# Dilated queries, keys and eight gate tiles by seven block products (Strassen) in an fp32 hybrid-attention layer

## The chip, the cores and the metric

The kernel runs on one core of one Trainium2 chip. The time is the device time of one execution of the program in microseconds (us), as the median of several runs. In this text, "faster" or "slower" means a difference of over 0.5% of the median before.

## What is computed

The layer takes x (1024 tokens by 1024 channels, fp32), normalises it, multiplies it by one wide input matrix and cuts the result into the operands of two attention mixers and two gates:

```python
h = rmsnorm(x, attn_norm_g)
proj = h @ w_in
(c_q, c_kv, k_rope, z_mla, q_dil, k_dil, v_dil, z_dil, g_mla, g_dil) = jnp.split(proj, ...)
a_out = mla_attention(...)                      # 8 heads, dense, 1024 by 1024 scores each
y_mla = (a_out * silu(z_mla)) @ w_o_mla
d_out = dilated_mixture(q_dil, k_dil, v_dil)    # 3 groups of 8 heads, rotary on q and k
y_dil = (d_out * silu(z_dil)) @ w_o_dil
merged = sigmoid(g_mla + b) * y_mla + sigmoid(g_dil + b) * y_dil
out = rmsnorm(x + merged @ w_out)
```

The dilated queries and keys are 2 x 1536 columns of `proj`, the two z and the two g are 2 x 512 and 2 x 1024 columns. In tiles of 128 columns that is 24 tiles of queries and keys, 8 of z and 16 of g (8 of g_mla, 8 of g_dil).

## The kernel before

**Numbers.** All matmuls are fp32 by three fp32r products: each operand is held as a high part and the remainder (`split`, L73 to L76: ScalarE casts the high part, another engine subtracts it), and `mm3` (L67 to L71) issues high x high, high x low and low x high. A projection tile (`proj_steps`) is 128 output columns by one half of the tokens (512): 8 chunks of the 1024 channels, 24 matmuls of 128x512, into one PSUM bank. One tile of 128 columns is therefore 48 such matmuls. The activations stay in SBUF as `hT_h` and `hT_l`; weights are loaded as `w_raw` (512 KB a tile), cast on ScalarE to `w_h` and subtracted on GpSimd to `w_l` (`wtile`).

**Stages.** (1) `latent_proj`. (2) `latents`, in which the latents are expanded for the dense mixer, together with the six calls of `dil_v` (values, 128x256 matmuls), whose matmuls fill the gaps of the latents. (3) `dil_qk`, 12 calls, each for two tiles (the two rotary halves of four heads): 96 matmuls of 128x512, then `rope` (L233: VectorE multiplies PSUM by cosine and sine, L234 and L235: GpSimd adds and subtracts), a split on ScalarE and GpSimd, and stores to DRAM (`s_dq`, `s_dk`). (4) `dil_attention`, (5) `mla_attention`, (6) the loop over the 16 tiles (8 column tiles by 2 halves) of `output` before the last product, (7) the last product with `w_out`.

**Fillers.** In stages 4 and 5 TensorE would wait for softmax, so a generator, `fillers`, hands out other matmuls: first the 24 tiles of z and g (16 steps of three matmuls each), then the output projection of the dilated mixer (64 steps), then three of the four parts of that of the dense mixer. `feed(n)` owes n steps at each of its call sites; `FEED` holds n for the sites, its last two numbers for the dense mixer: one after each 128-row score block (`s_mla`, L529) and one after each group of four transposes (`pt`, L543). There are 192 such calls. The generator can reach a point where it has to wait for finished heads (`mla_done`); its steps are then empty. What the fillers have not done of the output projection is left to stage 6, where each tile needs VectorE for a gate (L825), for the low part of the merged tile (`mg_l`) and for the low part of one piece of `w_out` (`wout_l`).

**Order.** The tile framework's scheduler fixes every engine's order of instructions when the program is built; on the chip each engine runs its list in order. Pools of SBUF and PSUM are a stack: a tile of a pool opened later may lie where a closed pool's tile lay, and then waits for its last reader.

Of the kernel before, what the change touches and what calls it, by code (L numbers as in the profile page):

```python
# [10 lines left out]
F32 = mybir.dt.float32  # L11
# [20 lines left out]
FEED = (1.9, 1.35, 1.2, 1.25, 2, 3, 1.1, 1.1)  # L32
# [6 lines left out]
T_ZM, T_QK = 0, 24  # L39

# [9 lines left out]
class Net:  # L50
# [16 lines left out]
    def mm3(self, out, lh, ll, rh, rl, start, stop):  # L67
        mm = self.nc.tensor.matmul
        mm(out, lh, rh, start=start, stop=False)  # L69
        mm(out, lh, rl, start=False, stop=False)  # L70
        return mm(out, ll, rh, start=False, stop=stop)  # L71
# [7 lines left out]
    def wtile(self, src, wp=None, n=8):  # L79
        raw = self.wp.tile([128, 8, 128], F32, name="w_raw")  # L80
        wp = wp or self.wp
        h = wp.tile([128, 8, 128], F32R, name="w_h")
        l = wp.tile([128, 8, 128], F32R, name="w_l")
        self.dma(raw[:, :n], src)
        self.split(raw[:, :n], h[:, :n], l[:, :n], self.nc.gpsimd)
        return h, l

    def proj_half(self, w, half, pool):

        return run_all(self.proj_steps(w, half, pool))  # L90

    def proj_steps(self, w, half, pool):

        ps = pool.tile([128, 512], F32, name="pj")
        t = slice(half * 512, half * 512 + 512)
        for kc in range(8):
            self.mm3(ps, w[0][:, kc], w[1][:, kc], self.hTh[:, kc, t], self.hTl[:, kc, t], kc == 0, kc == 7)
            if kc < 7:
                yield
        return ps  # L100
# [234 lines left out]
    def dil_v(self, g, quad, tp, pj):  # L335

        nc, a = self.nc, self.a
        w = []
        for kk in range(2):
            raw = self.wp.tile([128, 4, 256], F32, name="w_raw")  # L340
            wp = (self.wp, self.wpx)[kk]
            h = wp.tile([128, 4, 256], F32R, name="w_h")
            l = wp.tile([128, 4, 256], F32R, name="w_l")
            self.dma(raw, a["wv"][g * 2 + quad, kk])
            self.split(raw, h, l, nc.gpsimd)
            w.append((h, l))
        for t in range(8):
            ps = pj.tile([128, 512], F32, name="pj")[:, :256]
            for kc in range(8):
                wh, wl = w[kc // 4]  # L350
                sl = slice(128 * t, 128 * t + 128)
                self.mm3(ps, self.hTh[:, kc, sl], self.hTl[:, kc, sl], wh[:, kc % 4], wl[:, kc % 4], kc == 0, kc == 7)
            pv = ps.rearrange("p (h d) -> p h d", d=64)
            f = self.rcol[:, t:t + 1]
            if g < 2:
                st = tp.tile([128, 4, 2, 64], F32R, name="dv_st")
                nc.scalar.mul(st[:, :, 0], pv, f)
                nc.vector.scalar_tensor_tensor(out=st[:, :, 1], in0=pv, scalar=f, in1=st[:, :, 0].bitcast(F32), op0=ALU.mult, op1=ALU.subtract)
                x = slice(quad * 512, quad * 512 + 512)
                if g == 0:  # L360
                    dst = self.dv[0][128 * t + 64:128 * t + 192, x]
                else:

                    dst = self.dv[1].rearrange("(r m) x -> m r x", r=4)[32 * t:32 * t + 32, :, x]
                self.dma(dst, st.rearrange("p h a d -> p (h a d)"))
            else:
                st = tp.tile([128, 4, 64], F32, name="dv_s2")
                nc.scalar.mul(st, pv, f)
                self.dma(self.dv[2][128 * t:128 * t + 128, quad * 256:quad * 256 + 256], st.rearrange("p h d -> p (h d)"))

    def dil_qk(self, g, quad, which, tp, pj):

        nc, a = self.nc, self.a
        base = T_QK + (g * 2 + quad) * 4 + which * 2
        wa, wb = self.wtile(a["wt"][base]), self.wtile(a["wt"][base + 1], wp=self.wpx)
        if g < 2:
            st = [[tp.tile([128, S], F32R, name=f"dq_st{c}{p}") for p in range(2)] for c in range(2)]
        else:
            st = [[tp.tile([128, S], F32, name=f"dq_st{c}0")] for c in range(2)]
        for half in range(2):  # L380
            c512 = slice(half * 512, half * 512 + 512)
            pa, pb = self.proj_half(wa, half, pj), self.proj_half(wb, half, pj)
            o = self.rope(pa, pb, self.cos_d[:, c512], self.sin_d[:, c512], tp)
            for c in range(2):
                if g == 0:
                    self.split(o[c], st[c][0][:, c512], st[c][1][:, c512], nc.gpsimd)
                    continue
                if g == 1:
                    src = o[c].rearrange("p (m r) -> p r m", r=4)
                    dst = [x.rearrange("p (r m) -> p r m", r=4)[:, :, 128 * half:128 * half + 128] for x in st[c]]  # L390
                    self.split(src, dst[0], dst[1], nc.gpsimd)
                else:

                    src = o[c].rearrange("p (m b e) -> p e b m", b=8, e=2)
                    dst = st[c][0].rearrange("p (e b m) -> p e b m", e=2, b=8)[:, :, :, 32 * half:32 * half + 32]
                    for e in range(2):
                        nc.scalar.copy(out=dst[:, e], in_=src[:, e])
        off = 64 if (g == 0 and which) else 0
        dst = (self.dq if which == 0 else self.dk)[g]
        for c in range(2):  # L400
            for p in range(len(st[c])):
                for j in range(4):

                    self.dma(dst[quad * 4 + j, p, c, :, off:off + S], st[c][p][32 * j:32 * j + 32])
# [10 lines left out]
    def fillers(self, pj):  # L415
# [3 lines left out]
        with tc.tile_pool(name="zt", bufs=2, side="right") as tp:  # L419
            z_tile = lambda: tp.tile([128, 512], F32, name="zg_z")  # L420
            t_tile = lambda: tp.tile([128, 512], F32, name="zg_t")
            for i in [4, 5, 6, 7, 0, 1, 2, 3, *range(16, 24), *range(8, 16)]:
                w = self.wtile(a["wt"][T_ZM + i])
                for half in range(2):
                    c = slice(half * 512, half * 512 + 512)
                    ps = yield from self.proj_steps(w, half, pj)
                    z, t = z_tile(), t_tile()
                    nc.vector.tensor_tensor(out=z, in0=ps, in1=self.R[:, c], op=ALU.mult)  # L428
                    if i < 8:
                        nc.scalar.activation(out=t, in_=z, func=AF.Tanh, scale=0.5)  # L430
                        nc.gpsimd.tensor_tensor(out=t, in0=t, in1=z, op=ALU.mult)
                        nc.gpsimd.tensor_tensor(out=t, in0=t, in1=z, op=ALU.add)
                        self.dma(self.zs[i][:, c], t)
                    else:
                        nc.scalar.activation(out=t, in_=z, func=AF.Tanh, scale=0.5, bias=self.hb[:, i - 8:i - 7])
                        self.dma(self.gt[i - 8][:, c], t)
# [49 lines left out]
    def o_proj(self, i, dt, half, w, w0, js, br, t, pp, w3=None):  # L486
# [4 lines left out]
        for j in js:  # L491
            wh, wl = (x[:, dt if j == 3 and w3 else w0 + j] for x in (w3 if j == 3 and w3 else w))
# [303 lines left out]
    def output(self, pp):  # L796
        nc, a, tc = self.nc, self.a, self.tc
        v = nc.vector
        with tc.tile_pool(name="w3", bufs=1) as w3p, tc.tile_pool(name="wo", bufs=1) as wp, tc.tile_pool(name="mg", bufs=1) as mp:
            w3 = self.wtile(a["wom3"], wp=w3p)  # L800
# [64 lines left out]
    def run(self):  # L865
        tc, nc = self.tc, self.nc
        with ExitStack() as ctx:
# [23 lines left out]
            with tc.tile_pool(name="wpx", bufs=2, side="right") as self.wpx, tc.tile_pool(name="cosd", bufs=1, side="right") as dpool:  # L891
                z = dpool.tile([128, 8, 64], F32, name="zero")
                with tc.tile_pool(name="pj_a", bufs=NB_A, space=PSUM) as pj:
                    with tc.tile_pool(name="dvp", bufs=3) as vp, tc.tile_pool(name="lp", bufs=1) as lp, \
                            tc.tile_pool(name="pj_l", bufs=8 - NB_A, space=PSUM) as pl:
# [4 lines left out]
                        with tc.tile_pool(name="cosm", bufs=1) as mpool, tc.tile_pool(name="up", bufs=1) as lp:  # L900
# [5 lines left out]
                            for g in range(3):  # L906
                                for quad in range(2):
                                    self.dil_v(g, quad, vp, pj)
                    nc.vector.memset(z, 0.0)
# [3 lines left out]
                    with tc.tile_pool(name="dt", bufs=2, side="right") as tp:  # L913
                        for x in (self.cos_d, self.sin_d):
                            for half in range(2):
                                c = slice(512 * half, 512 * half + 512)
                                nc.gpsimd.tensor_tensor(out=x[:, c], in0=x[:, c], in1=self.R[:, c], op=ALU.mult)
                        for quad in range(2):
                            for g in range(3):
                                self.dil_qk(g, quad, 0, tp, pj)  # L920
                                self.dil_qk(g, quad, 1, tp, pj)
# [98 lines left out]
```

## Time and profile before

| | us |
|---|---|
| median of 3 runs (1336.35, 1343.12, 1337.54) | 1337.54 |
| the profiled execution | 1340.99 |
| its span, first to last instruction | 1339.2 |
| stage 1, 0 to 49.5 | 49.5 |
| stage 2, latents and values, 49.5 to 229.6 | 180.1 |
| stage 3, dilated queries and keys, 229.6 to 497.8 | 268.2 |
| stage 4, dilated attention, 497.8 to 822.7 | 324.9 |
| stage 5, dense attention, 822.7 to 1196.4 | 373.7 |
| stage 6, rest of the output projection, 1196.4 to 1243.4 | 47.0 |
| stage 7, product with `w_out`, 1243.4 to 1339.2 | 95.8 |

The cuts are the starts of the first `pj<-hT_h,w_h` (stage 3), `s_ps` (4), `s_mla` (5), the end of the last `av` (6) and the start of the first `pj<-wout_h` (7) on TensorE. In rows of the profile, PE is TensorE, PEld its weight load, DVE VectorE, ACT ScalarE, POOL GpSimd and SP the queue that issues the DMAs. The duration of a matmul in a row is its latency; matmuls overlap, and what one costs is the distance between starts.

### The profile page before, as it was taken

How to read it: one execution, taken by the hardware profiler on the slowest of the kernel's cores; microseconds unless marked ns; L12 is line 12 of the kernel's file. 1: busy time of each engine (PE TensorE's matmuls, PEld its weight loads, DVE VectorE, ACT ScalarE, POOL GpSimd, SP SyncE). 2: the span in 40 equal slices, each digit the busy share in tenths (PEclk: the TensorE clock that was granted, in tenths of full speed). 3: DMA queues.
4: the chain of work that ended last, by engine and by line, in shares of the span. 5: the costliest groups of instructions: out<-in, count | busy, mean ns of one | idle time of the engine just before them, and what ended most of it. 6: DMA issues, size and time to landing. Idle time of an engine off the chain costs nothing.

```text
span 1339.2 us, 19315 instructions
## 1 busy us (share of the span) xinstructions
PE 1275.4 (95%) x7101; PEld 1108.4 (83%) x7101; DVE 655.4 (49%) x1204; ACT 563.3 (42%) x1102; POOL 455.0 (34%) x302
## 2 busy tenths in 40 slices
PE   8989999999999999988989889999999999998998
PEld 8879999888888878877878777788888878886786
DVE  7483520222222224656576565656555556558622
ACT  6533332123322225545455453455554545444322
POOL 2251212576466634525422031212111022035522
PEclk9989999999999999989999999999999999999999
DMA  9747562585345535678777778545333463136322
GB/s 322 227 154 272 196 248 80 162 217 159 106 115 151 135 98 164 163 184 224 190 186 208 196 195 203 156 120 160 92 99 100 103 178 119 63 116 205 131 96 75
DMA packets 128253, 213.03 MB, mean 159 GB/s; under 512 B 36440, under 2 KB 65696, under 8 KB 126304
## 3 DMA queue, kind: packets, MB, share of 16 engines
q1 hardware_dynamic: 128160, 211.81, 54.6%
q8 instruction: 56, 0.92, 0.3%
q14 instruction: 37, 0.30, 0.1%
HBM read 143.01 MB, written 68.75 MB: 158 GB/s over the span
## 4 chain that ended last, share of the span: by engine, by line
PE 70%; DMA 9%; DVE 5%; issue 2%; SPq 1%; ACT 1%; POOL 1%; DVEq 0%; ACTq 0%; POOLq 0%
PE pj L69 17%; PE pj L70 16%; PE pj L71 16%; PE pt L543 4%; PE av L552 2%; PE av L551 2%; PE s_mla L69 2%; PE s_mla L71 2%; PE s_mla L70 2%; DMA s_sd<-av_t 2%; PE pt L642 2%; SPq L65 1%; PE av L663 1%; DMA op_a<-s_dk 1%; PE s_ps L698 1%
## 5 line engine op out<-in xcount | busy, mean ns | idle before, releaser
L69 PE MATMUL pj<-hT_h,w_h 128*128 128x512 f32 x768 | 315.0, 410 | 3.7 <-DVE zg_z L428 2.1
L76 POOL TENSOR_TENSOR w_l<-w_raw,w_h 128x1024 fp32r<-128x1024 f32 (+1 forms) x70 | 167.5, 2396 | 441.1 <-ACT w_h L75 371.4
L71 PE MATMUL pj<-hT_h,w_l 128*128 128x512 f32 x768 | 301.9, 393 | 0.0
L70 PE MATMUL pj<-hT_l,w_h 128*128 128x512 f32 x768 | 301.6, 393 | 0.0
L233 DVE TENSOR_TENSOR rope_m<-pj,cs_d 128x512 f32<-128x512 f32 x96 | 61.9, 686 | 241.1 <-PE pj L71 241.1
L76 DVE TENSOR_TENSOR pt_l<-pt,pt_h 128x512 fp32r<-128x512 f32 x192 | 131.6, 686 | 89.0 <-ACT pt_h L75 87.1
L71 PEld LDWEIGHTS pj<-hT_h,w_l 128*128 128x128 f32 x768 | 145.3, 189 | 31.5
L69 PEld LDWEIGHTS pj<-hT_h,w_h 128*128 128x128 f32 x768 | 145.8, 190 | 29.7 <-DVE zg_z L428 3.0
L75 ACT CAST pt_h<-pt 128x512 fp32r<-128x512 f32 x192 | 112.0, 584 | 130.0 <-PE pt L543 60.0
L70 PEld LDWEIGHTS pj<-hT_l,w_h 128*128 128x128 f32 x768 | 146.0, 190 | 24.4
L70 PE MATMUL pj<-w_l,hT_h 128*128 128x256 f32 x384 | 109.6, 286 | 0.0
L71 PE MATMUL pj<-w_h,hT_l 128*128 128x256 f32 x384 | 109.4, 285 | 0.0
L69 PE MATMUL pj<-w_h,hT_h 128*128 128x256 f32 x384 | 109.3, 285 | 0.0
L75 ACT CAST w_h<-w_raw 128x1024 fp32r<-128x1024 f32 (+1 forms) x70 | 72.3, 1034 | 74.5 <-PE pj L70 59.5
L529 DVE TENSOR_REDUCE m_nm<-s_mla 128x1 f32<-128x1024 f32 x64 | 78.0, 1221 | 32.6 <-PE s_mla L71 32.4
L608 ACT ACTIVATE p<-p,d_st 128x256 f32<-128x256 f32 x128 | 64.4, 505 | 60.5 <-DVE d_st L607 60.4
L532 ACT ACTIVATE p<-s_mla,m_nm 128x1024 f32<-128x1024 f32 x64 | 71.8, 1123 | 25.5 <-PE pt L543 19.2
L543 PE MATMUL pt<-consts,p 128*128 128x128 f32 x512 | 79.6, 276 | 0.0
L552 PE MATMUL av<-pt_l,op_c 128*128 128x256 f32 x256 | 67.2, 286 | 8.5 <-DVE pt_l L76 8.5
L69 PEld LDWEIGHTS pj<-w_h,hT_h 128*128 128x128 f32 x384 | 73.6, 192 | 1.1
L607 DVE CUSTOM_DVE_ANT_0 p<-s_ps,masks 128x256 f32<-128x256 f32 x128 | 51.0, 417 | 48.0 <-PE s_ps L635 27.3
L70 PEld LDWEIGHTS pj<-w_l,hT_h 128*128 128x128 f32 x384 | 73.7, 192 | 0.7
(232 smaller groups left out, 2548.4 us busy)
## 6 DMA issues: line engine op xcount, KB each, us to landing
w_raw<-wt SPq DMA_DIRECT2D x48, 512.0 KB, 4.7
op_b<-s_dq SPq DMA_DIRECT2D x32, 512.0 KB, 8.5
s_dq<-dq_st SPq DMA_DIRECT2D x80, 128.0 KB, 2.6
s_dk<-dq_st SPq DMA_DIRECT2D x80, 128.0 KB, 2.4
gate<-s_gt SPq DMA_DIRECT2D x34, 256.0 KB, 3.0
s_dv<-dv_st SPq DMA_DIRECT2D x32, 256.0 KB, 3.9
s_gt<-zg_t SPq DMA_DIRECT2D x32, 256.0 KB, 3.7
w_raw<-wv SPq DMA_DIRECT2D x12, 512.0 KB, 5.9
```

What stands on the lines that cost most here:

```text
L69: mm(out, lh, rh, start=start, stop=False)
L70: mm(out, lh, rl, start=False, stop=False)
L71: return mm(out, ll, rh, start=False, stop=stop)
L75: self.nc.scalar.copy(out=h, in_=raw)
L76: sub.tensor_tensor(out=l, in0=raw, in1=h.bitcast(F32), op=ALU.subtract)
L233: v.tensor_tensor(out=mi, in0=p, in1=tab, op=ALU.mult)
L529: v.tensor_reduce(out=nm[:, hh, qb:qb + 1], in_=s, axis=AX.X, op=ALU.max, negate=True)
L532: nc.scalar.activation(out=p, in_=s, func=AF.Exp, bias=nm[:, hh, qb:qb + 1], accum_out=den[:, hh, qb:qb + 1])
L543: self.anchor = nc.tensor.transpose(pt[:, o:o + 128], P[b2][:, 128 * kc:128 * kc + 128], self.ident)
L552: nc.tensor.matmul(a_out, vv[:, kc], pl[:, s], start=False, stop=kc == 7)
L607: nc.vector.tensor_tensor_reduce(out=p, in0=s, in1=mask, op0=ALU.add, op1=ALU.min, scale=-0.125, scalar=3e38, accum_out=nm)
L608: nc.scalar.activation(out=p, in_=p, func=AF.Exp, scale=-1.0, bias=nm, accum_out=den)
```

## The change

Two tiles of columns are computed together: the 1024 channels are cut into two halves, the 1024 tokens into two halves and the 256 columns into two tiles, so that a pair is a 2 by 2 block product. Instead of eight block products (8 x 4 chunks x 3 = 96 matmuls of 128x512), `block_pair` makes seven (84), in Strassen's form as Winograd wrote it: four sums of the blocks of x are built once for all pairs (`block_sums`: `s0` to `s3`, high and low), and for every pair four sums of weight blocks are made on GpSimd, in place in `w_raw` (`minus`). The seven weight operands are split in halves of the earlier tile size (128x512), ScalarE and GpSimd as before. The products go to four PSUM banks `st_a` to `st_d`; three copies on ScalarE (`copied`) and five additions on VectorE, which write to PSUM, put the four outputs together.

Done this way are the 12 calls of `dil_qk` and 8 of the 16 gate tiles (i = 8 to 15, those of g_mla) as 4 pairs, which leave the fillers and go into stage 3 after pairs 2, 5, 8 and 11. The rotation and the split of `dil_qk` now run on VectorE alone, in place in PSUM, and the four stores of a part become one DMA of 512 KB. The last two numbers of `FEED` go from 1.1 to 0.7. Pools move: `sums` and `bs` lie where the pools of the latents lay, and `dt`, which now holds two of the three pairs of `w_raw` in flight, lies where the values' staging pool `dvp` lay.

```diff
-FEED = (1.9, 1.35, 1.2, 1.25, 2, 3, 1.1, 1.1)
+FEED = (1.9, 1.35, 1.2, 1.25, 2, 3, 0.7, 0.7)
+ZG_PAIRS = ((8, 2), (10, 5), (12, 8), (14, 11))
...
+    def block_sums(self, sp, tp):
...
+        for kc in range(4):
...
+                    self.dma(x, a["xt"][i, :, c])
+                    nc.scalar.mul(x, x, self.ga[:, c:c + 1])
+            p.tensor_tensor(out=y[1, 1], in0=y[1, 0], in1=y[1, 1], op=ALU.add)
+            p.tensor_tensor(out=y[1, 0], in0=y[0, 0], in1=y[1, 0], op=ALU.subtract)
+            p.tensor_tensor(out=y[0, 0], in0=y[1, 1], in1=y[0, 0], op=ALU.subtract)
+            p.tensor_tensor(out=y[0, 1], in0=y[0, 1], in1=y[0, 0], op=ALU.subtract)
+            for i, x in enumerate((y[1, 1], y[0, 0], y[1, 0], y[0, 1])):
+                self.split(x, self.sh[i][:, kc], self.sl[i][:, kc], nc.vector)
...
+    def block_pair(self, first, tp, pp):
...
+            raw.append(self.wp.tile([128, 8, 128], F32, name="w_raw") if self.pairs % 3 == 0 else tp.tile([128, 8, 128], F32, name="w_raw", bufs=4))
+            self.dma(raw[i], a["wt"][first + i])
...
+        ps = {n: pp.tile([128, 512], F32, name=f"st_{n}") for n in "abcd"}
...
+        w1, w2 = operand(b[b11]), operand(b[b21])
+        minus(t1, b[0, 1], b11)
+        minus(t3, b[b22], (0, 1))
+        product("a", w1, hx(0, 0), True)
+        product("b", w2, hx(0, 1), True, True)
+        w1, w2 = operand(b[t1]), operand(b[t3])
+        minus(t2, b[b22], t1)
+        product("c", w1, sx(0), True)
+        u = copied("a")
+        v.tensor_tensor(out=ps["b"], in0=ps["b"], in1=u, op=ALU.add)
+        product("d", w2, sx(2), True)
+        w1, w2 = operand(b[b22]), operand(b[t2])
+        minus(t4, b[b21], t2)
+        u = copied("c")
+        t = tp.tile([128, 512], F32, name="st_t")
+        v.tensor_tensor(out=t, in0=ps["d"], in1=u, op=ALU.add)
+        product("a", w2, sx(1), False, True)
+        product("c", w1, sx(3), False, True)
+        product("d", operand(b[t4]), hx(1, 1), False, True)
+        u = copied("a")
+        for bank, x in (("a", t), ("c", u), ("d", u)):
+            v.tensor_tensor(out=ps[bank], in0=ps[bank], in1=x, op=ALU.add)
...
     def dil_qk(self, g, quad, which, tp, pp):
...
-            pa, pb = self.proj_half(wa, half, pj), self.proj_half(wb, half, pj)
-            o = self.rope(pa, pb, self.cos_d[:, c512], self.sin_d[:, c512], tp)
...
+            for x, y in zip(m, (pb, pa)):
+                v.tensor_tensor(out=x, in0=y, in1=sin, op=ALU.mult)
+            for x in o:
+                v.tensor_tensor(out=x, in0=x, in1=cos, op=ALU.mult)
+            for x, y, op in zip(o, m, (ALU.subtract, ALU.add)):
+                v.tensor_tensor(out=x, in0=x, in1=y, op=op)
...
-                for j in range(4):
-                    self.dma(dst[quad * 4 + j, p, c, :, off:off + S], st[c][p][32 * j:32 * j + 32])
+                self.dma(dst[quad * 4:quad * 4 + 4, p, c, :, off:off + S], st[c][p])
...
-            for i in [4, 5, 6, 7, 0, 1, 2, 3, *range(16, 24), *range(8, 16)]:
+            for i in [4, 5, 6, 7, 0, 1, 2, 3, *range(16, 24)]:
...
+                with tc.tile_pool(name="dt", bufs=1, side="right") as tp, tc.tile_pool(name="st", bufs=2, space=PSUM) as pp:
```

Counted in TensorE's list, stage 3 has 1368 matmuls of 128x512 now (1344 of the seven products and 24 of fillers) against 1176 before; the fillers have 696 in stage 4 both times, 339 against 642 in stage 5; stage 6 has 93 against 174. Together that is 192 fewer, 12 for each of 16 pairs. In stage 5, cut into its 32 blocks of 256 query rows, seven blocks have 3 fillers or none now (3, 3, 0, 0, 0, 0, 3), and three have 6; before every block had 15 to 24.

Three places in the order. First TensorE where stage 2 ends, before (the last rows of the values, then the first tile of queries):

```order
L69 MATMUL pj<-w_h,hT_h 128x256
L70 MATMUL pj<-w_l,hT_h 128x256
L71 MATMUL pj<-w_h,hT_l 128x256
L69 MATMUL pj<-hT_h,w_h 128x512
L70 MATMUL pj<-hT_l,w_h 128x512
L71 MATMUL pj<-hT_h,w_l 128x512
```

and now, with the first two block products (`st_a`, `st_b`):

```order
L73 MATMUL pj<-w_h,hT_l 128x256
L71 MATMUL st_a<-hT_h,w_h 128x512
L72 MATMUL st_a<-hT_l,w_h 128x512
L71 MATMUL st_b<-hT_h,w_h 128x512
L72 MATMUL st_b<-hT_l,w_h 128x512
L73 MATMUL st_a<-hT_h,w_l 128x512
```

The first products start on the high part of two operands, and the rows that need the low part `w_l` stand behind them.

Second, the DMA queue on SP at the same place, with what each entry waits for (DMAHW0 to 7 are the counters of completed DMAs that the queue's entries take in turn, the others count an engine's instructions). `s_dv` are the stores of the values, `w_raw<-wt` the loads of the weights of queries and keys. Before:

```order
L65 DMA s_dv_70<-dv_s_2206 128x256 [waits DMAHW1_49,Activation_49]
L65 DMA w_raw<-wt 128x1024 [waits DMAHW2_49,Pool_49]
L65 DMA s_dv_70<-dv_s_2246 128x256 [waits DMAHW3_49,Activation_49]
L65 DMA w_raw<-wt 128x1024 [waits DMAHW4_49,Pool_49]
L65 DMA s_dv_70<-dv_s_2274 128x256 [waits DMAHW5_49,Activation_49]
```

and now, the last stores of the values and the first loads:

```order
L67 DMA s_dv_70<-dv_s_2548 128x256 [waits DMAHW7_49,Activation_49]
L67 DMA s_dv_70<-dv_s_2576 128x256 [waits DMAHW0_49,Activation_49]
L67 DMA s_dv_70<-dv_s_2604 128x256 [waits DMAHW1_49,Activation_49]
L67 DMA w_raw<-wt 128x1024 [waits DMAHW4_49,DMAHW3_49,DMAHW5_49,DMAHW2_49,DMAHW6_49,DMAHW1_49,DMAHW7_49,DMAHW0_49,DVE_49]
L67 DMA w_raw<-wt 128x1024 x3
```

The loads stood among the stores and waited for one counter and GpSimd; the first load in this piece now stands behind the last store and waits for all eight counters. (Two loads, for the third pair, still stand earlier, among the stores of stage 2.)

Third, TensorE inside stage 5, behind a second matmul with the values (`av`) and a group of transposes (`pt`). Before, with the filler `pj<-brd_h,w_h` between the groups:

```order
L552 MATMUL av<-pt_l,op_c 128x256
L543 MATMUL pt<-consts,p 128x128 x4
L69 MATMUL pj<-brd_h,w_h 128x512
L70 MATMUL pj<-brd_l,w_h 128x512
L71 MATMUL pj<-brd_h,w_l 128x512
```

and now in one of the blocks without fillers:

```order
L661 MATMUL av<-pt_l,op_c 128x256
L652 MATMUL pt<-consts,p 128x128 x4
L71 MATMUL s_mla<-op_b,op_a 128x512
L72 MATMUL s_mla<-op_b,op_a 128x512
L73 MATMUL s_mla<-op_b,op_a 128x512
```

Where a filler stood, the next block's scores follow at once.

More of the change, by code (lines that the diff above doesn't have):

```diff
@@ L380, in dil_qk @@
+    def dil_qk(self, g, quad, which, tp, pp):
+        nc, a = self.nc, self.a
+        v = nc.vector
+        parts = 2 if g < 2 else 1
+        st = [[tp.tile([128, S], F32R if g < 2 else F32, name=f"dq_st{c}{p}") for p in range(parts)] for c in range(2)]
+        out = self.block_pair(T_QK + (g * 2 + quad) * 4 + which * 2, tp, pp)
         for half in range(2):
             c512 = slice(half * 512, half * 512 + 512)
-            pa, pb = self.proj_half(wa, half, pj), self.proj_half(wb, half, pj)
```

175 lines of the change are left out of this document (114 added, 61 removed).

## The prediction

> **What bounds the kernel now.** I read the page's first part, then the busy time of each engine by stage, then the spacing of TensorE's matmuls, then VectorE at the place where a stage could not get shorter with TensorE.
>
> ```profile
> PE 1275.4 (95%) x7101; PEld 1108.4 (83%) x7101; DVE 655.4 (49%) x1204; ACT 563.3 (42%) x1102; POOL 455.0 (34%) x302
> ...
> core 0: us, PE busy (x) PEld busy (x) DVE busy (x) ACT busy (x) POOL busy (x), PEclk, DMA share, GB/s
> 49.50:229.60 180.10, 172.91 (x1307) 166.35 (x1306) 74.38 (x162) 58.02 (x105) 43.13 (x23) 0.98 0.57 197
> 229.60:497.80 268.20, 266.73 (x1177) 220.53 (x1177) 61.87 (x96) 72.73 (x89) 162.34 (x104) 1.00 0.51 141
> 497.80:822.70 324.90, 299.76 (x1774) 261.81 (x1773) 192.21 (x483) 167.12 (x420) 109.32 (x85) 0.97 0.73 191
> 822.70:1196.40 373.70, 364.65 (x2074) 314.88 (x2074) 220.22 (x299) 187.16 (x327) 65.60 (x41) 0.99 0.43 120
> 1196.40:1243.40 47.00, 41.45 (x176) 32.26 (x174) 37.38 (x42) 20.12 (x33) 28.68 (x17) 1.00 0.55 185
> ```
>
> TensorE is the bound almost everywhere. Stage 3 (229.6 to 497.8) has 266.7 of 268.2 us busy, stage 5 364.7 of 373.7. Only in stage 6 is another engine close: VectorE 37.4 of 47.0 us. So matmuls taken out shorten the span where nothing else waits, and the question is where something does. Their price is the distance of their starts:
>
> ```profile
> 235.17 0.39 PE L69 MATMUL pj<-hT_h,w_h 128*128 128x512 f32 x1
> ...
> 241.06 0.39 PE L71 MATMUL pj<-hT_h,w_l 128*128 128x512 f32 x1
> ```
>
> The second is the 26th behind the first: 5.89 / 26 = 0.2265 us each, though a row lasts 0.39.
>
> **The seven products.** 192 matmuls fewer x 0.2265 = **-43.5 us**. A pair is 84 x 0.2265 = 19.03 us of TensorE. Do the other engines keep up with that?
>
> ```profile
> L233 DVE TENSOR_TENSOR rope_m<-pj,cs_d 128x512 f32<-128x512 f32 x96 | 61.9, 686 | 241.1 <-PE pj L71 241.1
> L76 POOL TENSOR_TENSOR w_l<-w_raw,w_h 128x1024 fp32r<-128x1024 f32 x65 | 157.9, 2432 | 401.6 <-ACT w_h L75 331.8 <-PE pj L70 26.3 <-DMA s_dv<-dv_s 18.3
> L234 POOL TENSOR_TENSOR rope_m<-rope_m,rope_m 128x512 f32<-128x512 f32 x26 | 33.6, 1293 | 88.4 <-DVE rope_m L233 88.4
> L76 POOL TENSOR_TENSOR dq_st<-rope_m,dq_st 128x512 fp32r<-128x512 f32 x32 | 45.0, 1431 | 0.0
> L75 ACT CAST w_h<-w_raw 128x1024 fp32r<-128x1024 f32 x65 | 68.1, 1050 | 68.7 <-PE pj L70 57.5 <-issue 7.6 <-PE pj L71 2.8
> L75 ACT CAST dq_st<-rope_m 128x512 fp32r<-128x512 f32 x32 | 27.9, 872 | 91.7 <-POOL rope_m L234 53.9 <-POOL rope_m L235 24.5 <-DMA s_dk<-dq_st 6.6
> L76 DVE TENSOR_TENSOR wout_l<-wo_raw,wout_h 128x512 fp32r<-128x512 f32 x16 | 16.7, 1051 | 8.2 <-DMA wo_raw<-w_out 4.2 <-ACT wout_h L75 4.0
> ```
>
> GpSimd has 7 splits of half the shown size (2.432 / 2 = 1.22) and 4 weight sums (1.29, as the adds of the rotation): 13.7 us a pair; at the 1.43 of the slowest row of its kind 15.7. ScalarE has 7 casts (half of 1.05), 3 copies and 4 casts (0.87 at most): 3.7 + 2.6 + 3.5 = 9.8. VectorE has 5 sums, 12 operations of the rotation and 4 subtractions, 21 x 0.686 = 14.4. All are under 19.03, so TensorE stays the bound. No row shows VectorE writing to PSUM; I take 0.686 because these operations read one operand from PSUM and one from SBUF as L233 does, and keep 1.05, the row with both operands in SBUF, as the other end. The additions of one pair fall beside the products of the next, on other banks: the last product of a pair waits for `st_t` (L454), which in VectorE's list stands behind the rotation of the pair before, some 16 operations or 11 us after that pair's end, and its turn comes after six products, 6 x 2.72 = 16.3 us. That is hidden with 5 us to spare; without the cover each 0.1 us more an operation would cost 1.6 us a pair once the 5 us are used up.
>
> The block sums (16 adds on GpSimd, 16 subtractions on VectorE, 32 operations on ScalarE, 16 loads of 256 KB) lie beside the values of stage 2, where VectorE has 74 of 180 us busy and GpSimd 43: 20 us on each is hidden, price 0.
>
> **The seam into stage 3.** This is the wait that is added. The first weights are loaded only after the last store of the values has landed, since their tile lies where the values were staged. Behind that load on SP's queue stand the loads for the second pair and nothing else that TensorE could use; TensorE itself has nothing else in its list.
>
> ```profile
> w_raw<-wt SPq DMA_DIRECT2D x48, 512.0 KB, 4.7
> ...
> s_dv<-dv_s SPq DMA_DIRECT2D x16, 128.0 KB, 1.7
> ...
> L368 ACT ACTIVATE dv_s<-pj,rcol 128x256 f32<-128x256 f32 x16 | 7.6, 475 | 29.4 <-PE pj L71 27.9 <-issue 1.5
> ```
>
> Eviction 0.48 + store 1.7 + load 4.7 + cast 0.53 + split 1.22 = 8.6 us before the products flow. Then the first pair's weights come as fast as GpSimd makes them: split, split, sum, sum, split puts the third operand 5 x 1.25 us after the first cast, where TensorE would want it after two products, 5.4: 1 to 2 us more. And the pause has an echo:
>
> ```profile
> 84.00:86.00 2.00, 0.91 (x5) 0.50 0.59 219
> 86.00:88.00 2.00, 2.00 (x11) 0.50 0.95 303
> 88.00:90.00 2.00, 2.00 (x12) 0.55 1.05 338
> ...
> 85.09 1.12 PE L277 MATMUL pj<-consts,lat 128*128 128x128 f32 x4 [5.74 <-DVE lat_l L281]
> ```
>
> After 5.74 us without work the granted clock is 0.50 for about 4.5 us (85.1 to 89.6). At half speed that is 2.2 us lost, which overlaps the slow first weights. **+10.8 us** together (7.4, where the first rows with `w_h` start, to 15, if four loads at once land late). [...]
>
> **The seam out of stage 3.** The filler's bank, the head's operands and the masks now wait for the end of the last pair, as `sums` lies where they go.
>
> ```profile
> 504.98 0.42 DVE L607 CUSTOM_DVE_ANT_0 p<-s_ps,masks 128x256 f32<-128x256 f32 x1 [6.04 <-PE pj L71]
> ...
> 505.47 0.39 PE L634 MATMUL s_ps<-op_a,op_b 128*128 128x256 f32 x1 [0.74 <-DVE d_st L607]
> ```
>
> The masks came late before, too: VectorE idled 6 us for them and TensorE, on fillers, 0.74. After the last matmul there are now seven operations of VectorE (4.8 us) where there were two (L233). **+2 us** (0 to 5). Stage 4 has the same list on TensorE: 0.
>
> **Stage 5.** Of the 192 fewer matmuls 303 leave this stage (-68.6 us) and 81 stage 6 (-18.3), while stage 3 gets 192 more (+43.5); together that is the -43.5 above. Does stage 5 follow?
>
> ```profile
> 960.00:1005.00 45.00, 45.00 (x261) 39.09 (x260) 24.36 (x32) 23.65 (x43) 6.09 (x3) 1.00 0.37 94
> 1005.00:1050.00 45.00, 45.00 (x263) 39.12 (x262) 24.57 (x33) 23.00 (x41) 3.69 (x2) 1.00 0.41 112
> ...
> L543 PE MATMUL pt<-consts,p 128*128 128x128 f32 x128 | 19.4, 273 | 0.0
> ```
>
> In these 90 us 128 transposes stand, 16 to a block: 8 blocks of 11.25 us, with 164 fillers, 20.5 x 0.2265 = 4.64 us a block. A block without fillers is 6.61 us of TensorE, against 6.1 of VectorE (48.9 / 8) and 5.8 of ScalarE (46.7 / 8), both with the fillers' own operations. With the mean of 10.6 fillers a block is 9.0 us, well over these; the sparse blocks are near balance. If a block takes at least 7.5 us, four empty ones lose 0.9 and three with three fillers 0.2: **+4 us**. The ends are 0 (6.61 holds) and +19 (no block under 9.0).
>
> **Stage 6.** 81 matmuls fewer are -18.3 us, but VectorE is in the way:
>
> ```profile
> 1205.53 0.83 DVE L76 TENSOR_TENSOR wout_l<-wo_raw,wout_h 128x512 fp32r<-128x512 f32 x1 [4.22 <-DMA wo_raw<-w_out]
> ...
> 1242.70 0.68 DVE L825 SCALAR_TENSOR_TENSOR gate<-gate,pj 128x512 f32<-128x512 f32 x1
> ...
> L76 DVE TENSOR_TENSOR mg_l<-gate,m 128x512 fp32r<-128x512 f32 x10 | 12.1, 1220 | 0.0
> L825 DVE SCALAR_TENSOR_TENSOR gate<-gate,pj 128x512 f32<-128x512 f32 x12 | 7.9, 677 | 0.0
> ```
>
> From its first low part to the last gate that TensorE needs there are 37.2 us: 16 `wout_l` x 1.05, 10 `mg_l` x 1.22, 12 gates x 0.68 make 37.1. So VectorE is already as long as TensorE here. With five PSUM banks TensorE's sixteenth tile needs the eleventh gate, and before that gate VectorE's list has 9 `wout_l`, 8 `mg_l` and 11 gates now: 26.7 us, 10.4 fewer. Of the 18.3 us some 8 are not realised, and 2 more where the second column block of the last product waits for the remaining `wout_l`: **+10 us** (5 to 15).
>
> **Sum.** -43.5 + 10.8 + 2 + 4 + 10 = **-16.7 us**. The profiled execution took 1340.99 us, 1.8 over its span; the sum makes it 1324.3. It lies 3.45 over the median 1337.54; the forecast for the median is **1320.8**.
>
> **Rivals.** (a) *All is hidden but the pause.* Stage 6 follows TensorE and no block is thin: -43.5 + 8.6, 1302.6. For it: stage 5 at 45.00 of 45.00 us busy. Against: stage 6's VectorE sum, which matches to 0.1 us. Chance 0.12.
> (b) *The thin fillers.* All blocks of stage 5 take 9.0 us: 19 instead of 4, so 1335.8, no change that can be told. For it: TensorE waits there for a chain through two engines; against: two score banks let the next block's scores run ahead. Chance 0.15.
> (c) *The seams are longer.* Their and stage 6's upper ends, 15, 5 and 15: +12.2, 1333. Chance 0.10.
> (d) *VectorE becomes the bound of stage 3.* Over 19.03 / 21 = 0.906 us an operation it is slower than TensorE. At 1.05 us, the row of `wout_l`, a pair takes 22.05 us; 12 pairs of queries and keys make +36.2: 1357, slower. For it: no row has VectorE writing to PSUM, and GpSimd, at 72%, runs beside it all the time. Against: L233 took 686 ns while GpSimd was busy 162 of 268 us. [...] Chance 0.13.
> That fewer matmuls are issued is settled by the order; no chance is left for the opposite.
>
> **Numbers.** The forecast has 0.50. About 0.5% (6.7 us) is what a measurement can tell from no change: faster is under 1330.9, slower over 1344.2. Faster: 0.50 + 0.12 = 0.62. The same: (b) and (c), less some 0.03 of their upper tail: 0.22. Slower: (d) and that tail: 0.16. The range reaches from (a), 1302, to just over the upper tail of (b) and (c), 1345, and leaves out (d) and little else. The forecast's own range is 1311 to 1331.
>
> **What would show it.** In the profile after: a pause of 8 to 9 us on TensorE behind the last value matmul, ended by GpSimd or ScalarE and traced to a `w_raw` load, with a clock of 0.5 behind it; stage 3 of about 324 us at 0.2265 us a matmul; `st_` operations of VectorE at about 0.69 us; stage 5 of about 309 us (373.7 - 68.6 + 4), with gaps in the sparse blocks; stage 6 of some 37 to 39 us with VectorE solid. Wrong it would be if VectorE's PSUM operations took over 0.9 us, if TensorE paused between the products of the later pairs, or if stage 5 kept over 325 us.

## The result, and the profile after

The changed kernel takes 1409.08 us (median), the kernel before 1338.05 us: 1.052 times as long, with a 95% interval of 1.048 to 1.056. The forecast was 1320.8 us with a range up to 1345. One of the four executions of the changed kernel took far longer than the rest (1560.64 us) and is left out of the ratio.

The page's first part:

```profile
PE 1269.8 (90%) x6909; PEld 1088.6 (77%) x6909; DVE 774.0 (55%) x1388; ACT 622.3 (44%) x1300; POOL 544.9 (39%) x430
```

The busy time of each engine by stage (the cuts are made by the same rows as before, stages 1 and 2 together and stage 3 from the first `st_a`):

```profile
core 0: us, PE busy (x) PEld busy (x) DVE busy (x) ACT busy (x) POOL busy (x), PEclk, DMA share, GB/s
0.00:235.70 235.70, 211.68 (x1497) 203.91 (x1497) 126.43 (x225) 110.00 (x222) 83.53 (x61) 0.97 0.68 232
235.70:621.90 386.20, 337.29 (x1369) 270.28 (x1369) 170.15 (x272) 128.88 (x244) 228.45 (x180) 0.92 0.35 115
621.90:953.20 331.30, 301.43 (x1773) 261.84 (x1772) 193.09 (x482) 169.29 (x434) 113.26 (x100) 0.95 0.73 192
953.20:1274.00 320.80, 303.38 (x1774) 259.54 (x1772) 213.35 (x292) 172.38 (x315) 64.27 (x53) 0.98 0.44 124
1274.00:1310.80 36.80, 26.66 (x94) 19.92 (x94) 30.76 (x36) 16.43 (x28) 23.12 (x15) 0.86 0.58 187
```

The matmuls are the forecast's: 6909, 192 fewer. Against before, stages 1 and 2 are 6.1 us longer, stage 3 118.0, stage 4 6.4, stage 5 is 52.9 shorter and stage 6 10.2, stage 7 is the same. Stage 3 was to grow by about 54 with its seam. There TensorE is idle for 49 of 386 us, at a mean granted clock of 0.92, no other engine is busy for more than 229, and the DMA engines are less busy than before (0.35, 0.51 before). So something waits there, and neither for an engine that is full nor for the DMA engines as a whole. TensorE's waits over the whole span (us in total, times, longest):

```profile
PE st_a L71 <- ACT st_c L434: 23.0, 4, 8.1
PE st_c L71 <- ACT st_c L434: 20.5, 4, 7.5
PE s_ps L743 <- DVE d_st L716: 12.4, 3, 11.3
PE av L661 <- DVE pt_l L78: 10.7, 15, 4.4
PE st_a L71 <- ACT w_h L77: 9.5, 1, 9.5
```

The last row is the forecast's pause, once. The first two are new: eight times, up to 8.1 us and 43.5 in all, the products wait for a copy on ScalarE that takes 0.6 us. To see why the copy is late, one such place is read backwards, TensorE first, then ScalarE's, VectorE's and SP's timelines (start, duration, idle before and what ended it):

```profile
298.28 0.79 PE L71 MATMUL st_c<-s_h,w_h 128*128 128x512 f32 x1 [7.49 <-ACT st_c L434]
```

```profile
282.43 0.59 ACT L77 CAST dq_st<-st_b 128x512 fp32r<-128x512 f32 x1 [6.21 <-DMA s_dq<-dq_st]
...
295.63 0.58 ACT L77 CAST dq_st<-st_a 128x512 fp32r<-128x512 f32 x1 [10.60 <-DVE st_a L503]
...
297.63 0.60 ACT L434 COPY st_c<-st_c 128x512 f32<-128x512 f32 x1
```

```profile
278.55 0.69 DVE L460 TENSOR_TENSOR st_d<-st_d,st_c 128x512 f32<-128x512 f32 x1
292.51 0.69 DVE L78 TENSOR_TENSOR dq_st<-st_b,dq_st 128x512 fp32r<-128x512 f32 x1 [13.27 <-DMA s_dq<-dq_st]
```

```profile
266.97 6.41 SPq L67 DMA_DIRECT2D s_dq<-dq_st  x4
274.22 4.84 SPq L67 DMA_DIRECT2D w_raw<-wt  x2
296.25 7.09 SPq L67 DMA_DIRECT2D s_dk<-dq_st  x4
```

The four stores of one pair are issued from 267.0 us. The next pair's first rotations are done, and their split is to go into the same staging tiles, of which `dt` now has one set. The rotation runs on VectorE alone, but the split does not: its high parts are still cast on ScalarE (L77), which is how the store reaches ScalarE's list. VectorE stands at the second half of the split for 13.3 us, until 292.5; ScalarE, in order, stands at its next cast of `dq_st` for 10.6; behind that cast is the copy `st_c`, and behind the copy are the products of the following pair. The store itself is the start of it: in the chain of waits it is what ended last (start, us).

```profile
268.83 23.59 DMA s_dq<-dq_st
297.25 14.25 DMA s_dk<-dq_st
...
341.77 22.18 DMA s_dq<-dq_st
...
455.49 22.17 DMA s_dq<-dq_st
```

These are 14 to 24 us, in a queue of four such stores, where the smaller stores of before took 2.4 to 2.6 us from issue to landing:

```profile
s_dq<-dq_st SPq DMA_DIRECT2D x80, 128.0 KB, 2.6
s_dk<-dq_st SPq DMA_DIRECT2D x80, 128.0 KB, 2.4
```

Stretches of 2 us after the change in which nothing else is loaded point to the reason (granted clock, DMA share, GB/s):

```profile
286.00:288.00 2.00, 1.00 0.26 106
288.00:290.00 2.00, 1.00 0.24 100
290.00:292.00 2.00, 1.00 0.26 104
```

The mean busy share of the 16 DMA engines is a quarter, all the time, and 100 to 106 GB/s go through; the row does not say whether four engines are busy or all of them for a quarter of the time. The 2 MB of a pair take 20 us at that rate. The theory that the experiments start from (A): the store of 128 rows by 4 KB, whose target is 4 heads by 32 rows, runs on 4 of 16 engines. Its rival (B): the in-order lists of ScalarE and VectorE with one set of staging tiles stall whatever the store does.

### The profile page after: what moved, and what is told of

It reads as the page before. It is cut to its first block, busy times and chain, and to the rows that moved or that the text cites. A ratio compares the mean times of both kernels' runs of the same rounds, so it can differ in the third digit from the quotient of the medians.

```text
span 1406.8 us, 19491 instructions
## 1 busy us (share of the span) xinstructions
PE 1269.8 (90%) x6909; PEld 1088.6 (77%) x6909; DVE 774.0 (55%) x1388; ACT 622.3 (44%) x1300; POOL 544.9 (39%) x430
## 4 chain that ended last, share of the span: by engine, by line
PE 52%; DMA 25%; DVE 12%; ACT 4%; issue 4%; SPq 2%; POOL 1%; ACTq 0%; DVEq 0%; POOLq 0%
PE pj L71 8%; DMA s_dq<-dq_st 8%; PE pj L73 8%; PE pj L72 8%; DMA s_dk<-dq_st 3%; PE pt L652 3%; DMA s_sd<-av_t 2%; PE av L661 2%; SPq L67 2%; PE s_mla L71 2%; PE av L660 2%; PE s_mla L73 1%; PE s_mla L72 1%; PE st_a L71 1%; PE st_c L71 1%
## 5 line engine op out<-in xcount | busy, mean ns | idle before, releaser
L78 POOL TENSOR_TENSOR w_l<-w_raw,w_h 128x512 fp32r<-128x512 f32 (+1 forms) x188 | 244.1, 1309 | 416.5 <-ACT w_h L77 346.6
L77 ACT CAST w_h<-w_raw 128x512 fp32r<-128x512 f32 (+1 forms) x188 | 113.8, 615 | 134.8 <-POOL w_raw L430 35.5
L77 ACT CAST pt_h<-pt 128x512 fp32r<-128x512 f32 x192 | 111.9, 583 | 91.2 <-PE pt L652 40.5
L71 PE MATMUL pj<-hT_h,w_h 128*128 128x512 f32 x256 | 111.5, 436 | 6.6 <-ACT dq_st L515 5.4
L72 PE MATMUL pj<-hT_l,w_h 128*128 128x512 f32 x256 | 103.9, 406 | 0.0
L73 PE MATMUL pj<-hT_h,w_l 128*128 128x512 f32 x256 | 103.7, 405 | 0.0
L430 POOL TENSOR_TENSOR w_raw<-w_raw 128x512 f32<-128x512 f32 x64 | 82.7, 1292 | 2.7
L661 PE MATMUL av<-pt_l,op_c 128*128 128x256 f32 x256 | 70.0, 297 | 10.8 <-DVE pt_l L78 10.7
L660 PE MATMUL av<-pt_h,op_c 128*128 128x256 f32 x256 | 72.2, 301 | 3.3 <-ACT pt_h L77 3.2
L73 PEld LDWEIGHTS pj<-w_h,hT_l 128*128 128x128 f32 x384 | 74.0, 193 | 0.8
L71 PE MATMUL st_c<-s_h,w_h 128*128 128x512 f32 x128 | 54.3, 424 | 20.5 <-ACT st_c L434 20.5
```

The costliest lines, as they stand in the source:

```text
L71: mm(out, lh, rh, start=start, stop=False, skip_group_check=skip)
L72: mm(out, lh, rl, start=False, stop=False, skip_group_check=skip)
L73: return mm(out, ll, rh, start=False, stop=stop, skip_group_check=skip)
L77: self.nc.scalar.copy(out=h, in_=raw)
L78: sub.tensor_tensor(out=l, in0=raw, in1=h.bitcast(F32), op=ALU.subtract)
L430: p.tensor_tensor(out=b[out], in0=x, in1=b[y], op=ALU.subtract)
```

## The experiments

**Four stores again.** The changed kernel, with

```diff
-                self.dma(dst[quad * 4:quad * 4 + 4, p, c, :, off:off + S], st[c][p])
+                for j in range(4):
+                    self.dma(dst[quad * 4 + j, p, c, :, off:off + S], st[c][p][32 * j:32 * j + 32])
```

> The changed kernel with the store of queries and keys as four DMAs of 32 rows again (128 KB each) in place of one of 128 rows (512 KB). Theory A, the store is the cause: four stores of one part land 22 to 24 us after their issue now, at about 104 GB/s with a quarter of the DMA engines' time busy, and the next part's casts wait for them in ScalarE's list, with the copies of the block products behind them. With four DMAs they land in under 6 us, stage 3 falls from 386 to about 325 us, the 6 us of stage 4 over before go too, and the time is 1409 - 61 - 6 = 1342 us (1334 to 1350). Theory B, the order on ScalarE and VectorE with one staging buffer is the cause whatever the store does: a dozen stalls of the casts stay, stage 3 stays over 365 us, the time over 1385.

Measured: 1346.77 us, 1.0075 times before (1.0055 to 1.0095). The stores in its page, and its stages 3, 4, 5 and 6:

```profile
s_dq<-dq_st SPq DMA_DIRECT2D x80, 128.0 KB, 2.5
s_dk<-dq_st SPq DMA_DIRECT2D x80, 128.0 KB, 2.6
```

```profile
232.30:557.80 325.50, 320.03 (x1368) 259.61 (x1369) 171.60 (x272) 131.26 (x244) 230.52 (x180) 0.98 0.48 136
557.80:887.50 329.70, 301.71 (x1773) 262.67 (x1771) 192.34 (x482) 169.14 (x434) 113.39 (x100) 0.95 0.74 194
887.50:1212.40 324.90, 305.20 (x1772) 261.30 (x1771) 213.29 (x292) 172.59 (x315) 64.66 (x54) 0.97 0.45 122
1212.40:1249.80 37.40, 26.89 (x93) 19.84 (x93) 31.32 (x36) 16.03 (x28) 21.90 (x14) 0.86 0.58 184
```

A holds: with landings of 2.5 us the same lists and the same single set of tiles stall nowhere between pairs, and stage 3 is 325.5 us. Of the 60.7 us by which it was longer, 43.4 are idle time of TensorE (48.9 against 5.5 us) and 17.3 are longer busy time of the same matmuls, at a mean granted clock of 0.92 against 0.98. Stage 4 kept most of the 6 us that were expected to go (329.7 against 331.3). The store is worth 1.052 - 1.0075, 4.5% or some 60 us. But even without it the change does not pay; the runs on fillers, gates and seams, below, take that up.

**Which dimension of the store.** Four DMAs of 128 KB as well, but cut along the tokens, so that each still goes to 4 heads by 32 rows:

```diff
-                self.dma(dst[quad * 4:quad * 4 + 4, p, c, :, off:off + S], st[c][p])
+                for j in range(0, S, 256):
+                    self.dma(dst[quad * 4:quad * 4 + 4, p, c, :, off + j:off + j + 256], st[c][p][:, j:j + 256])
```

> The changed kernel with its store cut into four DMAs of 128 KB, but along the tokens: each still goes to four heads by 32 rows, so its outermost dimension is 4, as that of the 512 KB store. Theory A1, a DMA is spread over the engines by its outermost dimension: it stays at about 104 GB/s and a quarter of the engines, and the time at 1409 (1390 to 1430). Theory A2, one large DMA is slow because of its size or because it is one: it behaves as four stores of 32 rows, 1342 (1334 to 1355).

Measured: 1402.79 us, 1.051 (1.046 to 1.055). The number and size of the DMAs are those of the run above, and the time is nearly that of the changed kernel. Where only these stores run, the share is a quarter again:

```profile
270.00:272.00 2.00, 1.00 0.27 92
272.00:274.00 2.00, 1.00 0.27 91
```

One thing differs besides: the rows of these DMAs are 1 KB long and not 4 KB. The next run keeps rows of 4 KB, so that their length can't be what slows it.

**Two heads at a time.** `dst[quad * 4 + j:quad * 4 + j + 2, ...]` for j = 0 and 2, from 64 rows of the tile.

> The changed kernel with each store of 512 KB cut into two DMAs of 256 KB, two heads by 32 rows each: the outermost dimension is 2. Theory A1 (a DMA is confined to as many engines as its outermost dimension divides into, and always to the same first ones): the stores run on two of 16 engines, at half the rate, about 52 GB/s and a share of 0.12 where nothing else runs; 2 MB of a call take 40 us instead of 20, and with 8 calls of four parts and 4 of two, stage 3 grows by up to 8 x 20 + 4 x 10 = 200 us: 1609 (1530 to 1640). Rival A3, each DMA is confined but different ones go to different engines: four and more in flight share the whole, 104 GB/s or more, and the time is 1409 or less.

Measured: 1587.29 us in a single run, beside 1336.46 for before. Two stretches of 4 us with only stores under way:

```profile
272.00:276.00 4.00, 1.00 0.13 53
276.00:280.00 4.00, 1.00 0.13 52
```

Half the rate and a share of an eighth (0.12 to 0.13 from 268 to 292 us), with eight such DMAs queued: their number does not raise it. A1 holds in what the rows show, a share of 0.24 to 0.27 for 4 heads and of 0.13 for 2; A2 and A3 fall. How many engines are behind these shares, and which, no run here shows. A larger store is not a better one here: one of 512 KB in a queue of four landed up to 24 us after its issue, one of 128 KB to a single head after 2.5.

**The store alone, in the kernel before.** Its four stores of a part made one, nothing else:

> The kernel before with the store of a part as one DMA of 512 KB, nothing else changed. Four such stores are issued for a call of 21.75 us, and at 104 GB/s they need 20 us, so they just keep up; the staging tiles have two buffers there. Theory A with the staging (a slow store hurts where the next pair needs the same buffer): little is lost inside stage 3, and 5 to 20 us where stage 4 has to wait for the last stores: 1341 to 1356. Rival, a store on a quarter of the engines delays everything behind it in the same engines' queues, loads of weights too: over 1370.

Measured: 1349.22 us, 1.011 (1.009 to 1.013), 15 us more. Stage 3 is 268.3 us as before: two sets of staging tiles are enough for 20 us of stores in a call of 21.75. Stage 4 is 14.1 us longer (339.0 against 324.9), and one wait of 16.7 us shows it, where all waits of its kind were 6.5 us before:

```profile
PE s_ps L632 <- DVE d_st L605: 22.1, 5, 16.7
```

In the kernel before, the load of the masks for stage 4 stands on SP's queue behind eight stores of the last keys (issued from 494.4 us, the masks at 500.3). That the masks come late here because the slow stores stand ahead of them is an inference: no row here shows when they land in this run. So the slow store costs 15 us in the kernel before, with two sets of tiles, and some 60 in the changed one, with one set. That the second set is what makes the difference is argued and not shown: the kernels differ in more than that, and the changed kernel was not run with the merged store and two sets.

**Fillers in stage 5.** Two runs with four stores, in which only the last two numbers of `FEED` differ from the first run, 0.5 and 1.1 instead of 0.7:

> Four stores as in the first run, and the last two numbers of FEED at 0.5 instead of 0.7: 288 fillers in stage 5 instead of 339, spread so that 27 of 32 blocks have 9, none has 0 (four have 0 with 0.7), and 144 matmuls in stage 6 instead of 93. Theory thin blocks: a block with few fillers has a floor of about 9 us, so stage 5 falls from 322 to about 305 and stage 6 grows from 37 to about 42: 12 us under the first run. Theory fillers do not matter there (stage 5's excess is single waits for DMAs): stage 5 falls by the 11.6 us of the matmuls alone, stage 6 grows by as much: the same as the first run within 4 us.

> Four stores as in the first run, and the last two numbers of FEED at 1.1 as before: 375 fillers in stage 5 instead of 339, but bunched: ten blocks in a row have none (four with 0.7). Theory thin blocks: at a floor of about 9 us a block the ten empty ones and the nearly empty ones lose some 33 us instead of 18, and the 36 fillers more add 8, of which stage 6 gives nothing back, as VectorE holds it: 20 us over the first run (12 to 28). Theory fillers do not matter there: stage 5 grows by 8 us and stage 6 stays: 4 to 8 us over the first run.

Measured: 1341.83 us (1.0035, 1.0013 to 1.0057) with 0.5, 1371.82 us (1.027, 1.023 to 1.030) with 1.1. Stages 5 and 6 of the run with 0.5, then of that with 1.1:

```profile
892.00:1208.20 316.20, 293.99 (x1730) 253.38 (x1730) 209.85 (x287) 171.70 (x313) 55.16 (x46) 0.97 0.44 120
1208.20:1246.70 38.50, 34.59 (x139) 26.37 (x138) 32.18 (x37) 17.27 (x31) 24.51 (x17) 0.96 0.63 201
```

```profile
892.50:1241.30 348.80, 320.53 (x1817) 274.68 (x1816) 220.41 (x297) 172.81 (x313) 69.29 (x57) 0.96 0.44 116
1241.30:1275.90 34.60, 21.08 (x49) 12.16 (x49) 29.38 (x34) 14.77 (x26) 21.35 (x14) 0.60 0.59 189
```

With 1.1 the theory of thin blocks gave 20 us and 25 were measured: 36 fillers more are 8.2 us of TensorE and stage 5 grows by 23.9. With 0.5 it gave 12 and 5 were measured: stage 5 falls by 8.7, less even than the 11.6 us of the 51 matmuls. So bunched fillers cost, but an even 9 a block is not enough to be rid of it: with 0.5 both theories miss, and these two runs leave open what the rest of stage 5's excess is. Stage 6 hardly follows the number of its matmuls in the three runs, with VectorE busy for 29.4, 31.3 and 32.2 us: 49, 93 and 144 matmuls take 34.6, 37.4 and 38.5 us, 1.1 us for the last 51, which would be 11.6 of TensorE.

**Only queries and keys.** Four stores, `ZG_PAIRS = ()`, the 8 gate tiles again at the end of the fillers' list and `FEED` at 1.1:

> The changed kernel with four stores, in which only the queries and keys are made by seven products: the 8 gate tiles are fillers again, and the last two numbers of FEED 1.1, so that every block of stage 5 has 15 to 24 fillers as before (633 in stage 5 instead of 339). TensorE has 48 matmuls of 128x512 more than with all pairs, 10.9 us. Theory, fillers were worth more where they stood: stages 5 and 6 lose nothing against before (19 and 9 us in the first run), stage 3 has 1008 + 24 matmuls of 0.230 us: 1347 + 11 - 19 - 9 = 1330 (1323 to 1336). Rival, the gates are as good in stage 3: 1347 + 11 = 1358.

Measured: 1332.30 us, 0.996 (0.994 to 0.999). Stages 5 and 6:

```profile
820.10:1191.00 370.90, 362.87 (x2074) 313.51 (x2074) 219.51 (x299) 189.84 (x342) 68.18 (x54) 0.99 0.43 121
1191.00:1235.80 44.80, 41.46 (x174) 32.29 (x174) 37.18 (x43) 19.54 (x35) 28.30 (x20) 1.00 0.61 195
```

It has 48 matmuls more than the run with all pairs, and is some 14 us faster. As fillers the eight gate tiles add 53 us to stages 5 and 6 (415.7 against 362.3); as pairs they added 77 to stage 3 (325.5 against 248.9 here), where TensorE is the bound (4 pairs of 84 matmuls at 0.2265 us are 76). The rest of the balance is lost elsewhere: stage 4 is 7.0 us longer here (336.7 against 329.7), stages 1 and 2 together 2.2. The rival, 1358, falls.

**The seam into stage 3.** The first pair's weights into the persistent pool (`self.pairs % 3 == 1` for `== 0`), with all pairs and with queries and keys only:

> The changed kernel with four stores, and the weights of the first of every three pairs (not of the third) in the persistent pool, so that those of the very first pair need not wait until the values' staging tiles are free. Theory seam: the 8.4 us pause of TensorE ahead of the first product and the half clock behind it (2.1 us) go: 10 us under the first run, 1337 (1333 to 1340). Rival, the first product waits for something else as well (the casts behind the evictions on ScalarE, the block sums on GpSimd): at most 3 us under the first run, 1344 or more.

> Both edits together: only queries and keys by seven products, four stores, fillers as before, the first pair's weights in the persistent pool. If both theories hold the gains add: 1330 - 10 = 1320 (1313 to 1328), under the kernel before. If one of them falls it is within 3 us of the other's run.

Measured: 1346.02 us (1.009, 1.007 to 1.011) and 1335.01 us (0.999, 0.997 to 1.002): no gain, the rival holds. TensorE's pause stayed, with another releaser, and ScalarE's timeline in the first of the two runs shows why:

```profile
PE st_a L71 <- ACT dv_s L376: 7.8, 1, 7.8
```

```profile
225.62 0.62 ACT L77 CAST s_h<-y 128x512 fp32r<-128x512 f32 x1 [3.58 <-POOL y L398]
226.14 0.47 ACT L376 ACTIVATE dv_s<-pj,rcol 128x256 f32<-128x256 f32 x1
...
229.56 0.47 ACT L376 ACTIVATE dv_s<-pj,rcol 128x256 f32<-128x256 f32 x1
```

The bank that the first product writes holds a tile of values until ScalarE evicts it (L376), at 229.6 us, 7 us after the last value matmul, because the eviction stands behind casts of block sums and of the first weights, and these wait for GpSimd. With the sums on VectorE (`p = nc.vector` in `block_sums`):

> The run with the first pair's weights in the persistent pool, and the 16 adds and subtractions of the block sums on VectorE instead of GpSimd. In that run the first product still waited 7.8 us, for a bank that ScalarE had not emptied: its eviction of the values stood behind casts of block sums, and these waited for GpSimd's sums until 230 us, 1.3 to 1.7 us each, with the splits of the first weights between them. Theory, the block sums on GpSimd set the seam: the pause falls from 7.8 us to under 3 and the half clock behind it goes: 6 to 8 us less, 1339 (1335 to 1342). Rival, the sums wait for their loads of x behind the stores on SP's queue, whoever adds: within 2 us of that run's 1346.

> Only queries and keys by seven products, four stores, fillers as before, the first pair's weights in the persistent pool, and the block sums on VectorE. By the theory that GpSimd's sums set the seam: 1335 - 7 = 1328 (1323 to 1331), under the kernel before; by the rival 1333 to 1337, no change.

Measured: 1341.32 us (1.005, 1.003 to 1.007), from 1.009, and 1328.73 us (0.9945, 0.9925 to 0.9966), from 0.999. The pause is 3.5 us in the first of these and 3.4 in the second, not quite under 3, but both times lie inside the range of the theory, and the rival falls.

**The seam out.** The last run once more, with the masks loaded by `nc.scalar.dma_start`:

> The same, and the load of the masks is issued from ScalarE's queue and not from SP's, where it stands behind eight stores of the last keys. Theory, the masks' place on SP's queue makes TensorE wait 8 us for VectorE's first masked scores at the start of stage 4: they come some 7 us earlier, and with the half clock 8 us go: 1320 (1315 to 1326). Rival, the last stores themselves or GpSimd's clearing of the probabilities behind them hold VectorE: within 2 us of the run without it.

Measured: 1324.77 us, 0.993 (0.991 to 0.995). The interval overlaps the run without it, and the wait in question is there still, so the 4 us are not put down to the edit. The chain shows what holds the masks now:

```profile
467.98 15.84 DMA op_c<-s_dv
483.84 2.49 DMA s_dk<-dq_st
...
486.63 3.98 DMA masks<-masks
```

A last store of the keys starts only when a load for stage 4 that was issued before it has landed, and the masks start when that store has. A place for the masks outside the freed pool was not tried. This run and the one without the masks' edit are faster than both kernels, by 0.55 and 0.7% against before in the median (the first interval reaches down to 0.3%): seven products for the queries and keys alone, four stores, block sums on VectorE.

## Why the prediction was wrong

**The step that failed is one that is missing.** The sum has no term for the store. The section on the change describes it ("the four stores of a part become one DMA of 512 KB"), and its diff opens the staging pool `dt` with one set of tiles (`bufs=1`), but the prediction's part on the seven products compares the busy time of engines only (GpSimd 13.7, VectorE 14.4, ScalarE 9.8 under 19.03 us), as if a list in order could not wait for a DMA. A quoted row already showed such a wait: L75's cast of `dq_st` was released by "DMA s_dk<-dq_st 6.6", with two sets of tiles and landings of 2.5 us. The store's landing should have been bounded on both sides like every other operation that the trace did not show. Measured, the landing was 14 to 24 us instead of 2.5, and with the lists that waited for it some 60 us of the result. None of the rivals held this either: the one on the other side, (d), named VectorE.

**Point by point**, in the run with four stores, in which that term is gone (span 1346.3 against 1339.2, +7.1 us, where the sum had -16.7). These are one profiled execution of each; by the medians of that session it is +10.4 us, so some 3 us have no place in the list:

- *Seven products, -43.5.* The count is right. VectorE's operations in PSUM take 0.69 us, as forecast, and rival (d) falls. What differs is the pace of TensorE without any wait: 218 matmuls in 50 us, 222 to 223 before, 2% or 6 us over stage 3.

```profile
300.00:350.00 50.00, 50.00 (x222) 1.00 0.57 155
350.00:400.00 50.00, 50.00 (x223) 1.00 0.38 106
```

```profile
350.00:400.00 50.00, 50.00 (x218) 1.00 0.40 116
400.00:450.00 50.00, 50.00 (x218) 1.00 0.54 147
```

- *Seam in, +10.8.* Measured is a pause of 8.4 us and a granted clock of 0.50 from 232.3 to about 236.5 us, as forecast (2 us). But the values end 5.6 us earlier than before, so that the first product comes only 2.6 us later. That was not foreseen, and why is open; some 2.4 us of it may be spread between executions, since the kernel before with the store alone changed comes to the same place at 227.2 us. The block sums, at price 0, were wrong: they and not only the load set the pause (the four runs on this seam).
- *Seam out, +2.* Stage 4 is 5 us longer, and TensorE waits 5.4 us more ahead of the first filler, for the copies of the last pair (L515), with a granted clock of 0.50 until about 554 us behind it: some 12 in all. The order of the last stores behind the next stage's loads was not read.
- *Stage 5, +4, with an end of 19.* 373.7 to 324.9 us is -48.8, where the matmuls gave -68.6: +19.8, of which 10.7 are more idle time of TensorE (19.7 against 9.0) and 9.1 longer busy time. This is rival (b) in size. Its mechanism is not confirmed. The empty blocks take 7.0 to 8.5 us from one first maximum to the next (7.5 was assumed, not 9.0), so they are not the floor. Of some 20 us in which TensorE is idle there, 11 stand at three places (3.7, 2.0 and 5.3 us), the last behind VectorE, which waited 6.3 us for a DMA that brings finished heads back from DRAM; after each the granted clock is about 0.5 for 3 to 7 us.

```profile
1131.06 0.69 DVE L532 TENSOR_TENSOR br_x<-br_x,gate 128x512 f32<-128x512 f32 x1 [6.33 <-DMA br_x<-s_ma]
```

- *Stage 6, +10.* 47.0 to 37.4 us is -9.6 where the matmuls gave -18.3: +8.7, right in size, and the three runs with different fillers bear out that fewer matmuls alone do not shorten the stage.

Together -43.5 + 6 + 2.6 + 2 + 12 + 19.8 + 8.7 is +7.6, against +7.1 measured.

So the run with four stores is rival (b) in size, the seam out of rival (c) (12 us, past its upper end of 5) and a pace of TensorE that no rival had; the store comes on top. Rivals (b) and (c) were given 0.15 and 0.10 as if only one of them could be true; each is a bound on another stage, and their prices add.

## What to carry to other kernels

Before merging several DMAs, look at the outermost dimension of the target that results (here 4 heads gave 100 to 106 GB/s and 2 heads 52 to 53), and price its landing; then ask which engine's list stands at the buffer that it must leave. Count a saving on TensorE stage by stage: work taken out of a stage where it filled gaps, or where another engine is as long, gives back only the rest (here 49 of 69 us and 10 of 18), and the same work put where TensorE is the bound costs in full (here 77 us for 76 of matmuls). Bounds on different stages that can all be true belong in the sum, not side by side as rivals.

## What was not expected of the hardware

Stores of 512 KB onto 4 heads by 32 rows, four in the queue, ran at 100 to 106 GB/s together, with a DMA share of a quarter; stores of 256 KB onto 2 heads, eight in the queue, at 52 to 53 with an eighth. If the quarter is four engines and the eighth two, that is about 26 GB/s an engine, an estimate by 104 over 4 and 53 over 2. Matmuls of the same shape came at 218 in 50 us while VectorE wrote other PSUM banks in place, against 222 to 223 where it only read them; whether that is the reason stays open.
